# First block of a two-block model: another form of the block compression, another order of the attention scores, and earlier bias loads

## The chip, the cores and the metric

The kernel runs on one core of a Trainium2 chip. The metric is the time of one execution on the device, in microseconds (us). Lower is better. Engines are named as in the profile: PE is TensorE, DVE is VectorE, ACT is ScalarE, POOL is GpSimd, SP is SyncE, whose queue here only issues transfers.

## The reference

Two transformer blocks run one after the other over 256 tokens of width 1024, in float32. The first block has a modulation from a condition vector, an mLSTM with four heads, sparse attention with eight heads in two key groups, and a mixture of 32 experts of which each token uses four. The second block has 16 more tokens, differential attention, a recurrent branch and a dense feed-forward layer. The change touches the sparse attention of the first block and the biases of its experts:

```python
def compress(k, pos_emb, w):          # one key per 32 tokens, stride 16
    idx = jnp.arange(n_cmp)[:, None] * CMP_STRIDE + jnp.arange(CMP_BLOCK)[None, :]
    blocks = k[:, idx] + pos_emb[None, None, :, None, :]
    return jnp.einsum('bilgd,lde->bige', blocks, w)

# sparse attention: compressed keys, selected blocks and a window, each with a
# softmax over q.k * scale + position bias of the head; three gates add them up
lc = jnp.einsum('bqghd,bigd->bqghi', qq, kc) * scale + bias_c
lw = jnp.einsum('bqghd,bkgd->bqghk', qq, kwb) * scale + bias

# expert: up = x @ w_up + b_up, swiglu, down = act @ w_down + b_down
```

With 256 tokens every block is selected, so the selected and the window branch see all earlier tokens.

## The kernel before

The program is written once through a layer that gives each engine its own list of instructions. The order in a list is set by a scheduler from the order in the source, so that what stands next to what is read from the lists and not from the source. `mixer` computes the modulation (`modulate`), then runs the list `it` of `mixer_items` (attention, mLSTM, output projection), then `close_mixer` and `router`. `moe` follows with the experts, `block2` with the second block.

A projection is a product of float32 split into a high and a low part: ACT casts a weight piece to `wh`, DVE or POOL computes the rest `wl`, and TensorE does three passes per row tile (lines 339 to 341, or 365 to 367 where tokens stand still). `F(key, n, then)` is one such projection of 128 columns, 24 passes; pieces are split three ahead (`LEAD1`). Between the projections stand the small steps of the attention. All PSUM tiles come from one pool of eight banks.

- `cin(n)` lays the 16 token offsets of the keys (n = 0) or values (n = 1) into `kx`. `compress(n)` (line 599) takes 16 products with the 128x128 weight `wcmp` as stationary operand, and streams 32 columns of `kx`. The output columns stand twice in the weight. DVE copies the sum to `pcs` and adds the position term to get `kcT` (line 605). `values_c` (line 612) transposes the compressed value, `values_c2` (line 621) spreads it.
- `scores(h)` has two products for head h (lines 682 and 684), over 64 rows: heads 0 to 3 use the lower half of the rows, heads 4 to 7 the upper. DVE adds the position bias `bt` and takes the maximum (line 691, four pieces per head), ACT takes exponentials. `turn(h)` transposes them (lines 705 to 707), `outs(h)` multiplies with the values (lines 724, 726).
- `cmp_scores` (line 637) has the scores of the compressed keys, `cmp_turn` (line 662) their transpose.
- `flips` (line 489) turns the position bias into `bt`.
- `row1(n)` is a part of the modulation (`mod_part`, line 502): 8 products with 32 stationary columns, in four column groups.
- `bias_part(c)` (line 1109) loads a piece of the expert biases to `bx` with ACT's queue and splits it into three bfloat16 parts with four casts on ACT and two differences on DVE.

SP's queue issues all the large weights in order (line 225, `load_w`, five buffers of 2 MB; line 1092 for the experts). A load waits there until its buffer is free, and those behind it wait too.

Of the kernel before, what the change touches and what calls it, by code (L numbers as in the profile page):

```python
# [9 lines left out]
F32 = mybir.dt.float32  # L10
# [4 lines left out]
ALU = mybir.AluOpType  # L15
# [99 lines left out]
def host_layout(i):  # L115
# [47 lines left out]
    o["wcmp"] = np.concatenate([wc, wc], 4).reshape(P, 4096)  # L163
# [31 lines left out]
class Kernel:  # L195
# [215 lines left out]
    def modulate(self, pc):  # L411
# [3 lines left out]
        sel = self.selm = pa.tile([P, 12], F32, name="selm")  # L415
        nc.gpsimd.memset(sel, 0.0)
        for j in range(4):
            nc.gpsimd.affine_select(sel, sel, pattern=[[-1, 12]], compare_op=ALU.not_equal, fill=1.0, base=-32 * j,
                                    channel_multiplier=1)
# [90 lines left out]
    def mixer_items(self, sx):  # L510
# [64 lines left out]
        def keys(n):  # L575
            return lambda po: nc.scalar.copy(kk[:, n], po)
# [99 lines left out]
        def scores(h):  # L676
            g, j = h // 4, h % 4

            def f():
                s = slice(64 * g, 64 * g + 64)  # L680
                p1 = self.ps(f"ps_a{h}")
                nc.tensor.matmul(p1, qa[s, j, P:T1], kkf[s, :], start=True, stop=True)
                p0 = self.ps(f"ps_b{h}")
                nc.tensor.matmul(p0[:, :T1], qa[s, j, 0:P], kk[s, :, 0:P], start=True, stop=True)
                e = B["e", h] = tx(f"e{h}", [P, 768], "e", 2)
                mx = tx(f"mx{h}", [P, 2, 2], "mx", 2)
                sm = B["sm", h] = tx(f"sm{h}", [P, 2, 2], "sm", 4)
                pieces = [(p1, 256 * b, T1, 256 * b, 1, b, bt[:, h, :]) for b in range(2)]
                pieces += [(p0, 128 * b, P, 512 + 128 * b, 0, b, bt[:, h, P:T1]) for b in range(2)]
                for ps, po, w, o, tt, b, bias in pieces:  # L690
                    nc.vector.tensor_tensor_reduce(e[:, o : o + w], ps[:, po : po + w], bias, scale=1.0, scalar=NEG,
                                                   op0=ALU.add, op1=ALU.max, accum_out=mx[:, tt, b : b + 1])
                nc.vector.tensor_scalar(mx, mx, -1.0, None, op0=ALU.mult)
                for ps, po, w, o, tt, b, bias in pieces:
                    nc.scalar.activation(e[:, o : o + w], e[:, o : o + w], AF.Exp, bias=mx[:, tt, b : b + 1],
                                         accum_out=sm[:, tt, b : b + 1])
            return f
# [103 lines left out]

        def load_gains():
# [82 lines left out]
        def T(key, off, n, xs, then, order=tuple(range(KT))):  # L885
            return [p if i % 2 else p[:2] + (pool,) for i, p in enumerate(self.lin_t(key, off, n, xs, then, None, order))]
# [9 lines left out]
        it += T("wins", 0, 280, xs, values) + [self.flips] + F(W0, 0, keys(0)) + F(W0, 1, keys(1)) + [gates2, compress(1), values_c]  # L896
        it += F(W1, 0, queries(0)) + [compress(0), scores(0), values_c2] + F(W1, 1, queries(1)) + [scores(4), row1(4)]
        it += F(W1, 2, queries(2)) + [turn(0)] + F(W1, 3, queries(3)) + [cmp_scores, scores(1), turn(4)]
        it += F(W2, 0, qkin(0)) + [cmp_turn, scores(5)] + F(W3, 0, qkin(4)) + [cmp_out, turn(1), outs(0), outs(4), row1(5)]
        it += F(W2, 1, qkin(1)) + [scores(2), outs(1)] + F(W3, 1, qkin(5)) + [turn(5), scores(6), row1(6)]  # L900
        it += F(W2, 2, qkin(2)) + [outs(5), turn(2), scores(3)] + F(W3, 2, qkin(6)) + [outs(2), turn(6), scores(7)]
        it += F(W2, 3, qkin(3)) + [outs(6), turn(3)] + F(W3, 3, qkin(7)) + [decay(0), outs(3), row1(7)]
        it += so_[0:2] + [turn(7)] + so_[2:4] + [decay(1), outs(7)] + so_[4:8] + [row1(8)] + vm_[0:4] + [row1(9)]
        it += vm_[4:8] + [show, load_gains, mixed(0), decay(2), row1(10), mixed(1), decay(3), turn_cat(4), turn_cat(5)]
        it += [row1(11), mixed(2), turn_cat(6), turn_cat(7), rows, mixed(3), end_att, bias(0), rows2]
        it += [turn_cat(0), turn_cat(1), bias(1), turn_cat(2), turn_cat(3), row2(10), row2(11), load_x]
# [1109 lines left out]
```

## Time and profile before

| | |
|---|---|
| median of three runs | 1950.04 us (1944.28 to 1952.6) |
| profiled execution | 1948.96 us, span 1947.3 us |
| PE busy | 1746.0 us, 90% of the span |
| DVE, ACT, POOL busy | 811.6, 570.7, 264.4 us |
| DMA | 557.72 MB, mean 286 GB/s |
| granted TensorE clock, mean | 0.937 |

The first 260 us are the first block without its experts, up to about 1190 us the experts run, and then the second block. Busy shares over the whole span mix these three. A granted clock of 1.00 is 2.4 GHz, 0.50 is 1.2 GHz. Spans of matmuls are modelled and overlap, so the distance from one start to the next tells more than the length of one. The trace counts two passes for a float32 product, which the instruction lists count as one.

### The profile page before, as it was taken

Reading aid. Unit: us, or ns where it says so; the run is one execution under the profiler, and the core shown is the slowest. Engines: PE = TensorE matmul, PEld = TensorE weight load, DVE = VectorE, ACT = ScalarE, POOL = GpSimd, SP = SyncE. Lnnn points to the kernel's source line nnn. Section 1 sums busy time; section 2 is a strip of 40 time slices with the busy share of each in tenths; the row PEclk is TensorE's granted clock in tenths of the full one; section 3 lists DMA queues with packets and bytes.
Section 4 is the critical chain, followed back from the end, with each engine's and each line's share of the span. In section 5 each row is a group of like instructions: output and inputs, shape, how many; then the busy total and the mean of one; then the engine's idle time right before and its main releaser. Section 6 shows DMA issues by size and latency. Waiting matters only on the chain.

```text
span 1947.3 us, 34253 instructions
## 1 busy us (share of the span) xinstructions
PE 1746.0 (90%) x14547; PEld 1239.9 (64%) x14548; DVE 811.6 (42%) x1804; ACT 570.7 (29%) x1128; POOL 264.4 (14%) x259
## 2 busy tenths in 40 slices
PE   6999979965999997699999766979999999789998
PEld 3877743433543543354254434878999998789998
DVE  3364552211122222122121214577666557876653
ACT  3454521100111110011010102435444446354442
POOL 2213110000000000000000001051233102323320
PEclk7899989987999999899999977888999999799999
DMA  9447869999999999999999998210443452225441
GB/s 384 181 183 270 307 269 430 426 427 425 393 426 427 427 426 427 427 425 428 427 426 427 427 427 349 98 52 36 173 173 133 149 222 93 82 87 188 175 149 52
DMA packets 42697, 557.72 MB, mean 286 GB/s; under 512 B 4788, under 2 KB 5964, under 8 KB 8360
## 3 DMA queue, kind: packets, MB, share of 16 engines
q1 hardware_dynamic: 39920, 548.67, 68.7%
q0 software_dynamic: 1200, 4.29, 0.6%
q10 hardware_dynamic: 1416, 2.49, 0.4%
q8 instruction: 116, 1.90, 0.4%
q14 instruction: 45, 0.37, 0.1%
HBM read 554.37 MB, written 1.06 MB: 285 GB/s over the span
## 4 chain that ended last, share of the span: by engine, by line
PE 56%; DMA 12%; DVE 5%; ACT 1%; issue 1%; ACTq 0%; POOL 0%; DVEq 0%; POOLq 0%
DMA we<-wexp 12%; PE ps_lin L339 9%; PE ps_lin L340 9%; PE ps_lin L341 9%; PE ps_l L1293 6%; PE ps_u L1293 6%; PE ps_d L1293 6%; PE ps_g L1259 2%; PE ps_c L1356 2%; DVE qk L1765 1%; PE ps_at L1336 1%; PE nm0ss L1473 0%; PE ps_rqb L1784 0%; PE ps_ri L1659 0%; PE ps_pg L1321 0%
## 5 line engine op out<-in xcount | busy, mean ns | idle before, releaser
L339 PE MATMUL ps_lin<-xhi,wh 128*128 128x272 f32 (+1 forms) x1024 | 301.9, 295 | 0.5 <-ACT xhi L1403 0.5
L340 PE MATMUL ps_lin<-xlo,wh 128*128 128x272 f32 (+1 forms) x1024 | 298.0, 291 | 0.4 <-DVE xlo L1404 0.4
L341 PE MATMUL ps_lin<-xhi,wl 128*128 128x272 f32 (+1 forms) x1024 | 298.0, 291 | 0.0
L1293 PE MATMUL ps_d<-we,at 128*32 128x256 f32 (+1 forms) x2048 | 219.7, 475 | 47.6 <-DMA we<-wexp 38.1
L1293 PE MATMUL ps_l<-we,xg 128*32 128x256 f32 (+1 forms) x2048 | 214.0, 454 | 30.6 <-DMA we<-wexp 29.7
L1293 PE MATMUL ps_u<-we,xg 128*32 128x256 f32 (+1 forms) x2048 | 211.9, 452 | 29.1 <-DMA we<-wexp 29.1
L339 PEld LDWEIGHTS ps_lin<-xhi,wh 128*128 128x128 f32 x1024 | 198.0, 194 | 2.5 <-ACT xhi L1403 0.8
L340 PEld LDWEIGHTS ps_lin<-xlo,wh 128*128 128x128 f32 x1024 | 198.0, 193 | 0.9 <-DVE xlo L1404 0.6
L341 PEld LDWEIGHTS ps_lin<-xhi,wl 128*128 128x128 f32 x1024 | 198.1, 193 | 0.0
L1293 PEld LDWEIGHTS ps_d<-we,at 128*32 128x32 f32 (+1 forms) x2048 | 89.2, 126 | 163.8 <-issue 94.5
L1293 PEld LDWEIGHTS ps_l<-we,xg 128*32 128x32 f32 (+1 forms) x2048 | 87.4, 120 | 139.7 <-issue 92.4
L1293 PEld LDWEIGHTS ps_u<-we,xg 128*32 128x32 f32 (+1 forms) x2048 | 85.5, 120 | 132.7 <-issue 77.5
L1360 DVE TENSOR_TENSOR hT<-hT,ps_c 128x512 f32<-128x512 f32 x128 | 79.3, 682 | 131.7 <-PE ps_c L1356 131.7
L1379 POOL TENSOR_TENSOR hT<-hT,g 128x1024 f32<-128x1024 f32 x1 | 3.3, 3257 | 943.2 <-DVE ssm L1377 943.2
L1422 ACT CAST wh<-wgu 128x1024 fp32r<-128x1024 f32 x88 | 92.2, 1049 | 121.9 <-PE ps_lin L340 119.3
L1425 DVE TENSOR_TENSOR wl<-wgu,wh 128x1024 fp32r<-128x1024 f32 x88 | 108.2, 1231 | 41.9 <-ACT wh L1422 41.9
L1305 DVE TENSOR_SCALAR gl<-ps_u 128x512 f32<-128x512 f32 (+1 forms) x36 | 20.3, 572 | 222.1 <-PE ps_u L1297 222.1
L1337 ACT COPY at<-ps_at 128x512 f32<-128x512 f32 (+1 forms) x36 | 17.4, 493 | 305.7 <-PE ps_at L1336 304.9
L339 PE MATMUL ps_lin<-ahi,wh 128*128 128x272 f32 (+1 forms) x352 | 100.5, 286 | 0.0
L341 PE MATMUL ps_lin<-ahi,wl 128*128 128x272 f32 (+1 forms) x352 | 99.9, 284 | 0.0
L340 PE MATMUL ps_lin<-alo,wh 128*128 128x272 f32 (+1 forms) x352 | 99.8, 283 | 0.0
L1422 ACT CAST wh<-win 128x1024 fp32r<-128x1024 f32 (+1 forms) x72 | 60.9, 855 | 117.9 <-PE ps_lin L340 115.2
(675 smaller groups left out, 2931.5 us busy)
## 6 DMA issues: line engine op xcount, KB each, us to landing
we<-wexp SPq DMA_DIRECT2D x192, 2048.0 KB, 27.0
wgu<-wgu SPq DMA_DIRECT2D x22, 2048.0 KB, 7.8
win<-win SPq DMA_DIRECT2D x14, 2048.0 KB, 8.1
wada<-wada SPq DMA_DIRECT2D x12, 2048.0 KB, 8.3
wdn<-wdn SPq DMA_DIRECT2D x16, 1408.0 KB, 6.1
wout<-wout SPq DMA_DIRECT2D x6, 2048.0 KB, 7.7
wint<-wint SPq DMA_DIRECT2D x2, 2048.0 KB, 11.2
wcmpNone<-wcmp SPq DMA_DIRECT2D x1, 2048.0 KB, 22.7
```

Source lines behind the costliest of these rows:

```text
L339: nc.tensor.matmul(po[:m, :nn], hi[:, a], xh[k], start=(k == 0), stop=False)
L340: nc.tensor.matmul(po[:m, :nn], hi[:, a], xl[k], start=False, stop=False)
L341: nc.tensor.matmul(po[:m, :nn], lo[:, a], xh[k], start=False, stop=(k == nk - 1))
L1259: nc.tensor.matmul(p, self.x[:, tt, k * P : k * P + P], oh[:, tt], start=(tt == 0), stop=(tt == 1))
L1293: nc.tensor.matmul(dst[b][s], lhs(k, b), ws[k // 4][:, o : o + wd], start=(k == 0 and b % per == 0), stop=False)
L1305: nc.vector.tensor_scalar(gl[i], pu[i], 7.0, 0.5, op0=ALU.min, op1=ALU.mult)
L1336: nc.tensor.transpose(pt[:, c * P : c * P + P], li[i][:, c * P : c * P + P], self.ident)
L1356: nc.tensor.matmul(pc[s][:, (tt - t0) * wd : (tt - t0) * wd + wd], gt[b][rows[s], tt * P : tt * P + P], y[b // per][rows[s], (b % per) * w ...
L1360: nc.vector.tensor_tensor(a, a, pc[s].rearrange("p (a b) -> p a b", a=per), op=ALU.add)
L1422: nc.scalar.copy(hi, src)
L1425: nc.vector.tensor_tensor(lo, src, hi.bitcast(F32), op=ALU.subtract)
L1765: nc.vector.tensor_tensor(B["qk"][:, i], B["qk"][:, i], z, op=ALU.add)
```

## The change

- Compression: the weight `wcmp` no longer repeats its columns (1 MB and no longer 2). The 32 columns of `kx` are the stationary operand, the 64 output columns stream, and product l writes to the column group of 32 that l modulo 4 names. DVE copies the four partial sums, twice side by side, to `cp`. A new step `compress2` adds and transposes them with one product with the selection matrix `selm`, which is widened from 12 to 32 columns. From there on all is as before.
- Scores: `scores(j)` issues both products of head j and of head 4+j, first the two large ones, then the two small, and then their DVE and ACT steps. `e` has three buffers, not two.
- Biases: the six pieces are loaded by `load_bias(c)` into the memory of `bt` (four, by SP's queue) and further ones by ACT's queue, ahead of `bias_part`.
- The list `it` is ordered anew around these steps.

```diff
-    o["wcmp"] = np.concatenate([wc, wc], 4).reshape(P, 4096)
+    o["wcmp"] = wc.reshape(P, 2048)
...
         def compress(n):
...
                 for l in range(16):
-                    o = (n * 16 + l) * P
-                    nc.tensor.matmul(pc[:, 0:32], w[:, o : o + P], kx[:, n, l].rearrange("p g i -> p (g i)"),
-                                     start=(l == 0), stop=(l == 15))
+                    o = (n * 16 + l) * 64
+                    q = 32 * (l % 4)
+                    nc.tensor.matmul(pc[q : q + 32, 0:64], kx[:, n, l].rearrange("p g i -> p (g i)"), w[:, o : o + 64],
+                                     start=(l < 4), stop=(l >= 12))
+                cp = B["cp", n] = tx(f"cp{n}", [P, 2, 64])
+                nc.vector.tensor_copy(cp, pc[:, 0:64].unsqueeze(1).to_broadcast([P, 2, 64]))
+            return f
+
+        def compress2(n):
+            def f():
+                pc = self.ps(f"ps_cmt{n}")
+                nc.tensor.matmul(pc[:, 0:32], B["cp", n].rearrange("p a b -> p (a b)"), self.selm, start=True, stop=True)
...
+        def scores(j):
...
+                for g in range(2):
+                    s = slice(64 * g, 64 * g + 64)
+                    p1 = self.ps(f"ps_a{4 * g + j}")
+                    nc.tensor.matmul(p1, qa[s, j, P:T1], kkf[s, :], start=True, stop=True)
+                    pss.append([p1])
+                for g in range(2):
+                    s = slice(64 * g, 64 * g + 64)
+                    p0 = self.ps(f"ps_b{4 * g + j}")
+                    nc.tensor.matmul(p0[:, :T1], qa[s, j, 0:P], kk[s, :, 0:P], start=True, stop=True)
+                    pss[g].append(p0)
+                for g in range(2):
+                    h = 4 * g + j
...
+                    e = B["e", h] = tx(f"e{h}", [P, 768], "e", 3)
...
+        def load_bias(c):
+
+            def f():
+                self.bx[c] = b2[0:96, 512 * (c % 4) : 512 * (c % 4) + 512]
+                (nc.sync if c < 4 else nc.scalar).dma_start(self.bx[c], d["bexp"][:, c * 512 : c * 512 + 512])
+            return f
...
-        it += T("wins", 0, 280, xs, values) + [self.flips] + F(W0, 0, keys(0)) + F(W0, 1, keys(1)) + [gates2, compress(1), values_c]
-        it += F(W1, 0, queries(0)) + [compress(0), scores(0), values_c2] + F(W1, 1, queries(1)) + [scores(4), row1(4)]
+        it += T("wins", 0, 280, xs, values) + [self.flips] + F(W0, 0, keys(0)) + [compress(1)] + F(W0, 1, keys(1))
+        it += [gates2, compress2(1), compress(0), values_c]
+        it += F(W1, 0, queries(0)) + [compress2(0), scores(0), values_c2] + F(W1, 1, queries(1)) + [row1(4)]
...
     def bias_part(self, c):
...
-            b = self.pr.tile([96, 512], F32, name=f"bx{c}", tag="bx", bufs=2)
+            b = self.bx[c]
...
-            nc.scalar.dma_start(b, self.d["bexp"][:, c * 512 : c * 512 + 512])
```

On PE, between the key projections and the first query projection, before the change (`ps_ac` is the gates' transpose, `ps_cmp` the compression, `ps_vc` the compressed value's transpose, `ps_lin` the projection):

```order
L565 MATMUL ps_ac<-ident,mr 128x4
L599 MATMUL ps_cmp_671<-cat,wcmpNone 128x32 x16
L612 MATMUL ps_vc<-ident,kcT 16x128
L339 MATMUL ps_lin_702<-hhi,wh_614 128x256
L340 MATMUL ps_lin_702<-hlo,wh_614 128x256
```

and with the change (`ps_cmt` is the selection product of `compress2`):

```order
L565 MATMUL ps_ac<-ident,mr 128x4
L610 MATMUL ps_cmt_690<-selm,cp_648 128x32
L601 MATMUL ps_cmp_696<-wcmpNone,cat 32x64 x16
L622 MATMUL ps_vc<-ident,kcT 16x128
L339 MATMUL ps_lin_725<-hhi,wh_614 128x256
L340 MATMUL ps_lin_725<-hlo,wh_614 128x256
```

The values' compression moved forward, to the second key projection (one of its 16 products among that projection's first passes, 15 before the next projection), and the keys' compression took its place.

On PE, between the first and the second query projection, before the change (`ps_a` and `ps_b` are a head's scores, `ps_rv` is `values_c2`):

```order
L599 MATMUL ps_cmp_732<-cat,wcmpNone 128x32 x16
L682 MATMUL ps_a_753<-kk,qa 128x512
L684 MATMUL ps_b_755<-kk,qa 128x256
L621 MATMUL ps_rv<-vc,rep 128x128
L339 MATMUL ps_lin_778<-hhi,wh_648 128x256
```

and with the change:

```order
L610 MATMUL ps_cmt_755<-selm,cp_713 128x32
L693 MATMUL ps_a_761<-kk,qa 128x512
L693 MATMUL ps_a_763<-kk,qa 128x512
L698 MATMUL ps_b_765<-kk,qa 128x256
L698 MATMUL ps_b_767<-kk,qa 128x256
L631 MATMUL ps_rv<-vc,rep 128x128
L339 MATMUL ps_lin_802<-hhi,wh_667 128x256
```

Head 4 moved to head 0. Pairs (2, 6) and (3, 7) stand in the same way; in pair (1, 5) four products of `cmp_scores` stand after the first `ps_a` and five of `mod_part` before the second `ps_b`.

In SP's queue, from the mLSTM's weights (`wint`) on, with the change (`wada` is the modulation, `wout` the output projection; before the change the rows are the same without line 824):

```order
L225 DMA wint1_120<-wint 128x4096
L824 DMA bt_140<-bexp 96x512 x2
L225 DMA wint0_124<-wint 128x4096
L225 DMA wada8_126<-wada 128x4096
L225 DMA wada7_122<-wada 128x4096
L824 DMA bt_140<-bexp 96x512 x2
L225 DMA wada9_128<-wada 128x4096
L225 DMA wada11_132<-wada 128x4096
L225 DMA wada10_130<-wada 128x4096
L225 DMA wout0_134<-wout 128x4096
```

Four bias loads moved into this queue from ACT's.

## Rows read from the trace of the kernel before

**Rows 1.** Busy time by stage; columns: stretch, length, each engine, granted clock, DMA.

```profile
94.30:160.00 65.70, 64.88 (x477) 51.58 (x477) 43.60 (x157) 36.06 (x107) 14.05 (x11) 1.00 0.51 197
160.00:250.00 90.00, 89.03 (x505) 66.46 (x503) 46.03 (x113) 47.26 (x91) 21.66 (x19) 0.96 0.73 275
250.00:260.00 10.00, 1.49 (x6) 1.35 (x6) 9.04 (x74) 1.30 (x4) 6.83 (x36) 0.50 0.14 42
260.00:1190.00 930.00, 810.31 (x7692) 387.31 (x7696) 196.49 (x431) 108.30 (x269) 0.00 (x0) 0.94 1.00 423
1190.00:1947.30 757.30, 705.40 (x5430) 678.73 (x5427) 482.62 (x941) 341.03 (x578) 196.62 (x144) 0.95 0.35 130
```

**Rows 2.** Waits, PE 72 to 260 us and SP's queue: total us, times, longest.

```profile
PE ps_rank L996 <- DVE sel L989: 7.7, 1, 7.7
PE ps_pc L662 <- DVE lc L657: 0.8, 1, 0.8
...
SPq L1092 <- DVE gate L1002: 20.4, 1, 20.4
```

**Rows 3.** Busy time of projections before and after the first compression, columns as above.

```profile
66.00:72.00 6.00, 6.00 (x50) 5.74 (x48) 1.37 (x2) 2.92 (x6) 1.91 (x3) 1.00 0.99 403
77.45:82.60 5.15, 5.15 (x25) 5.15 (x26) 0.97 (x2) 0.62 (x1) 0.00 (x0) 0.50 0.00 0
...
89.90:94.30 4.40, 4.40 (x26) 4.17 (x25) 1.81 (x6) 2.49 (x9) 1.33 (x2) 0.67 0.71 302
```

**Rows 4.** PE's timeline around the compressions: start, length, line, product, shapes, passes, wait.

```profile
72.45 4.09 PE L599 MATMUL ps_cmp<-cat,wcmpNone 128*128 128x32 f32 x32
77.42 0.37 PE L612 MATMUL ps_vc<-ident,kcT 128*16 128x128 f32 x1 [0.89 <-DVE kcT L605]
...
82.65 3.85 PE L599 MATMUL ps_cmp<-cat,wcmpNone 128*128 128x32 f32 x32
86.43 2.07 PE L682 MATMUL ps_a<-kk,qa 64*128 64x512 f32 x2
...
89.28 0.79 PE L621 MATMUL ps_rv<-vc,rep 16*128 16x128 f32 x2
```

**Rows 5.** PE's timeline, scores of head 2 and what follows.

```profile
127.73 1.12 PE L682 MATMUL ps_a<-kk,qa 64*128 64x512 f32 x2
...
129.22 0.88 PE L724 MATMUL ps_y<-vs,pr 128*128 128x64 f32 x6
```

**Rows 6.** PE's timeline of other forms, and loads of L502 (ns min/median/max).

```profile
62.84 3.60 PE L489 MATMUL ps_fl<-hank,flip 128*128 128x512 f32 x8
...
104.23 0.96 PE L637 MATMUL ps_cx<-kcT,qa 64*128 64x16 f32 x14
...
120.98 0.78 PE L724 MATMUL ps_y<-vs,pr 128*128 128x64 f32 x6
...
177.19 0.39 PE L366 MATMUL ps_lin<-wl,hhi 128*128 128x512 f32 x1
177.41 0.39 PE L367 MATMUL ps_lin<-wh,hlo 128*128 128x512 f32 x1
177.73 1.92 PE L502 MATMUL ps_modr<-wada,sc 128*32 128x512 f32 x16
...
L502 PEld LDWEIGHTS ps_modr<-wada,sc x128: 106/110/110, 95.8 to 201.1; 128*32 128x32 f32 x128
```

**Rows 7.** Waits of PE from 0 to 72 us, and PE's timeline at 193 us.

```profile
PE ps_mod L502 <- DMA wada<-wada: 2.7, 3, 1.5
PE ps_lin L366 <- DVE wl L1427: 1.5, 2, 1.0
...
192.85 3.63 PE L502 MATMUL ps_modr<-wada,sc 128*32 128x512 f32 x30
```

**Rows 8.** DVE's instructions of L691 (ns min/median/max, first and last start, form).

```profile
L691 DVE CUSTOM_DVE_ANT_0 e<-ps_a,bt x16: 408/420/425, 88.5 to 151.5; 128x256 f32<-128x256 f32 x16
L691 DVE CUSTOM_DVE_ANT_0 e<-ps_b,bt x16: 276/286/292, 89.4 to 152.4; 128x128 f32<-128x128 f32 x16
```

More of the change, by code (lines that the diff above doesn't have):

```diff
@@ L674, in mixer_items @@
         kkf = kk.rearrange("p b t -> p (b t)")
-        def scores(h):
-            g, j = h // 4, h % 4
+        def scores(j):
             def f():
[L680 to L696, printed above, removed]
@@ new lines, in f @@
+                pss = []
+                for g in range(2):
[8 more added lines that the diff above has]
+                    pss[g].append(p0)
@@ new lines, in f @@
+                for g in range(2):
+                    h = 4 * g + j
+                    p1, p0 = pss[g]
+                    e = B["e", h] = tx(f"e{h}", [P, 768], "e", 3)
+                    mx = tx(f"mx{h}", [P, 2, 2], "mx", 2)
+                    sm = B["sm", h] = tx(f"sm{h}", [P, 2, 2], "sm", 4)
+                    pieces = [(p1, 256 * b, T1, 256 * b, 1, b, bt[:, h, :]) for b in range(2)]
+                    pieces += [(p0, 128 * b, P, 512 + 128 * b, 0, b, bt[:, h, P:T1]) for b in range(2)]
+                    for ps, po, w, o, tt, b, bias in pieces:
+                        nc.vector.tensor_tensor_reduce(e[:, o : o + w], ps[:, po : po + w], bias, scale=1.0, scalar=NEG,
+                                                       op0=ALU.add, op1=ALU.max, accum_out=mx[:, tt, b : b + 1])
+                    nc.vector.tensor_scalar(mx, mx, -1.0, None, op0=ALU.mult)
+                    for ps, po, w, o, tt, b, bias in pieces:
+                        nc.scalar.activation(e[:, o : o + w], e[:, o : o + w], AF.Exp, bias=mx[:, tt, b : b + 1],
+                                             accum_out=sm[:, tt, b : b + 1])
@@ L800, in mixer_items @@
         grow = {4: kk.rearrange("p a b -> p (a b)"), 5: vs.rearrange("p a b -> p (a b)")}
+        def load_bias(c):
[3 more added lines that the diff above has]
+            return f
+        self.bx = {}
         def load_gains():
@@ L900, in mixer_items @@
[L900 to L903, printed above, removed]
+        it += T("wins", 0, 280, xs, values) + [self.flips] + F(W0, 0, keys(0)) + [compress(1)] + F(W0, 1, keys(1))
@@ new lines, in mixer_items @@
+        it += [gates2, compress2(1), compress(0), values_c]
+        it += F(W1, 0, queries(0)) + [compress2(0), scores(0), values_c2] + F(W1, 1, queries(1)) + [row1(4)]
+        it += F(W1, 2, queries(2)) + [turn(0)] + F(W1, 3, queries(3)) + [cmp_scores, turn(4), scores(1)]
+        it += F(W2, 0, qkin(0)) + [cmp_turn, turn(1)] + F(W3, 0, qkin(4)) + [cmp_out, outs(0), outs(4), row1(5)]
+        it += F(W2, 1, qkin(1)) + [scores(2), turn(5), outs(1)] + F(W3, 1, qkin(5)) + [row1(6), turn(2)]
+        it += F(W2, 2, qkin(2)) + [outs(5), turn(6), scores(3)] + F(W3, 2, qkin(6)) + [outs(2), outs(6)]
@@ L904, in mixer_items @@
+        it += F(W2, 3, qkin(3)) + [turn(3)] + F(W3, 3, qkin(7)) + [decay(0), outs(3), row1(7)]
+        it += so_[0:2] + [turn(7)] + so_[2:4] + [decay(1), outs(7)] + [load_bias(c) for c in range(4)] + so_[4:8] + [row1(8)] + vm_[0:4] + [row1(9)]
         it += vm_[4:8] + [show, load_gains, mixed(0), decay(2), row1(10), mixed(1), decay(3), turn_cat(4), turn_cat(5)]
         it += [row1(11), mixed(2), turn_cat(6), turn_cat(7), rows, mixed(3), end_att, bias(0), rows2]
-        it += [turn_cat(0), turn_cat(1), bias(1), turn_cat(2), turn_cat(3), row2(10), row2(11), load_x]
+        it += [turn_cat(0), turn_cat(1), load_bias(4), bias(1), turn_cat(2), turn_cat(3), load_bias(5), row2(10), row2(11), load_x]
```

6 lines of the change are left out of this document (2 added, 4 removed).

## The prediction, made before the changed kernel ran

> **What bounds the kernel now.** I read the program by stages first. From 260 to 1190 us the DMA share is 1.00 at 423 GB/s: the experts' weights set the pace there, and TensorE waits for them. From 1190 us on TensorE is busy 705 of 757 us. Neither stage is touched by the change beyond a few neighbours trading places, so I count both as fixed lengths that begin when the stage before them lets them [rows 1]. What lets them begin is the router: the queue that issues the expert weights stood 20.4 us waiting for the gates, and the DMA share is 0.14 just before they come [rows 1, 2]. The first block is therefore in series with all the rest: a microsecond taken off it is a microsecond off the end.
>
> Inside the first block TensorE is the limit. From 94.3 to 250 us it is busy 154 of 156 us [rows 1], and the waits say the same: 0.8 us for the compressed scores, then 7.7 us for the router's choice, which is the end of the block [rows 2]. So each step of the change is priced by the TensorE time it takes away or adds before 250 us.
>
> The clock comes with it. The projection products run at one pass per 0.120 us (50 in 6.00) at a granted clock of 1.00, which is 2.4 GHz. Right after the first compression the granted clock is 0.50, 1.2 GHz, and a pass takes 0.206 us (25 in 5.15) [rows 3]. What TensorE did before each fall was a compression: 32 passes, each with a load of 128 columns for a stream of only 32.
>
> **The change part by part.** *Compression.* Before, the first compression with the wait behind it lasts from 72.45 to 77.42, 4.97 us, 0.89 of it the wait for the key that VectorE finishes. The second lasts from 82.65 to 86.43, 3.78 us [rows 4]. That is 8.75 us. Now the 16 products of each have the 32 tokens as stationary operand, stream 64 columns, and stand in four column groups. The trace counts two passes per float32 product, so there are 8 rounds of four. A round costs at least its stream: 512 columns take 3.60/8 = 0.45 us, so 64 take 0.056 and a compression 0.45 us. If the groups did not overlap, 32 loads of 0.110 us would give 3.5 us. The nearest row is the modulation, also 32 stationary columns in four groups: 16 passes of 512 columns in 1.92 us, where 0.45 each would be 7.2, so the groups do overlap [rows 6]. A load (0.110) outlasts the 0.056 stream, so I take 0.11 per round, 0.9 us per compression. Each then needs one product with the selection matrix, two passes with 128-column loads at 4.09/32 = 0.13 us [rows 4], 0.26 us. Going into the column groups costs 0.32 - 0.23 = 0.09 us (177.41 to 177.73, against 0.23 between the passes before; [rows 6]). The new order has six such borders, 0.5 us, because one product of the first compression stands alone among the key products. New total: 1.8 + 0.5 + 0.5 = 2.8 us, a gain of 5.9. Ends: 6.8 if only the stream counts, 0.8 if nothing overlaps. The wait of 0.89 us I count as gone: the second compression (0.9 us) now stands between the selection product and the transpose that needs its key. Without that cover it is back.
>
> The Trainium skill, "TensorEngine Tiling (Array Packing)", Key Properties, says that a change of tiling mode drains the engine, which speaks against splitting a compression. The 0.09 us of the trace is what that drain costs here, and the sum has it. "TensorE: Matmul & The Clock Gate", LDWEIGHTS, gives a load as its columns over 1.2 GHz, which would be 27 ns for 32 columns. The trace has 106 to 110 ns for float32 [rows 6]. By the page the gain would be near the upper end, 6.8.
>
> *The clock.* If it stays at 1.00, the query products behind the first compression gain 25 x (0.206 - 0.120) = 2.15 us and the 26 passes from 89.9 to 94.3 gain 4.40 - 3.12 = 1.28 [rows 3]. The first head's score products take 89.28 - 86.43 = 2.85 us there, and 129.22 - 127.73 = 1.49 at full clock [rows 4, 5], another 1.36. Sum 4.8. I expect it to stay. The products with 64-column streams on the whole array (6 in 0.78 us, [rows 6]) sit in a stage whose granted clock is 1.00 throughout [rows 1], and the new compression streams 64 columns for 0.9 us at a time. Ends: 0 if it falls as now, and -2 if the early first compression makes it fall among the key products, which have the full clock today.
>
> *Scores in pairs.* A head's two products take 1.49 us on half of the rows [rows 5]. Heads j and 4+j lie on different halves. Products that alternate between the halves go 14 passes in 0.96 us, 0.069 each, against 0.13 for passes with the same load on all rows [rows 6], so they do run side by side. In the new order three of the four pairs stand next to each other, and each saves 1.49 us: 4.5. The pair (1, 5) has compressed scores and modulation products in between, and I give it nothing. Ends: 0 and 6.
>
> *Bias loads.* Two of six stood first in ScalarE's queue and ran among the first block's weights. 0.39 MB at 0.423 MB/us [rows 1] is 0.9 us of DMA time, and TensorE waits 2.7 us for those weights [rows 7], so I take 0.9 (0 to 0.9). Four now stand in SP's queue and wait until VectorE has read the position bias. Behind the last two stand three modulation weights, both output weights and the experts'. VectorE's last such read starts at 152.4 [rows 8], and the modulation that is first among those held is needed at 192.85 [rows 7], so nothing is late. The 24 bias casts on ScalarE are the same ones, 16 of them now before the output weights' casts. ScalarE is busy 47 of 90 us there [rows 1]: nothing, or up to 2 us if the output product has to wait for a cast.
>
> *Flips.* Two of the four bias flips now stand among the value products, where TensorE waits 1.5 us for VectorE's splits [rows 7]. I take 0.5 (0 to 1.5).
>
> *New waits.* A pair gives VectorE 4 x 0.42 + 4 x 0.29 = 2.8 us in one piece, where it had 1.4 [rows 8]. Behind it are the splits that the next projection needs, and behind the exponentials the transposes, which for heads 1 and 2 now come one projection (3 us) after their scores. VectorE is busy 43.6 of 65.7 us in that stage [rows 1], and the stage gets shorter. Ends: 0, and 1.4 us at each of four pairs, 5.6. I take 1.5, nearer to none, since splits are made three parts ahead.
>
> Sum: 5.9 + 4.8 + 4.5 + 0.9 + 0.5 - 1.5 = 15.1 us. The profiled execution took 1948.96 us, 1.08 below the median of 1950.04. That gives 1933.9 in its terms and 1934.9 in the median's: **1935 us**.
>
> **Rivals.** *The clock falls all the same.* For it: products over only 64 rows and short streams remain near the compression. Against it: the stage of the other short streams keeps 1.00. Then 4.8 are missing: 1940.
>
> *VectorE takes over.* Both ends of the new waits' term: 4 us more, 1939. For it: the long pieces. Against: it has a third of the stage free.
>
> *The groups don't do what they say.* If passes in different column groups run one after the other, a compression stays at 3.5 us, 5.1 of the 5.9 go, and the clock goes with them, since its cause is back: 15.1 - 5.1 - 4.8 = 5.2, 1945. Against it stands the modulation's row.
>
> *Slower than before: starved pairs.* If TensorE waits at the pairs and the clock falls after each, a fall costs about 2.2 us (its price after the first compression) and a wait about 1.4. Four pairs and two compressions make 6 x 3.6 = 21.6 us, against a gain of 15.1 - 4.8 + 1.5 = 11.8 without the clock and without the waits: 1960. It decides from the fourth such place on (14.4). Against it: the clock holds 1.00 from 94.3 to 160 today with a wait of 0.8 us inside.
>
> **How the numbers follow.** About 0.5% is what a measurement of this kernel can tell from no change: 9.7 us, so a time below 1940.3 counts as faster. My forecast (1928 to 1939) has 0.60. The clock's fall has 0.16, half of it on either side of the bound. VectorE has 0.09, two thirds on the faster side. Groups that don't overlap have 0.10, all within 0.5%. Starved pairs have 0.05. Faster: 0.60 + 0.08 + 0.06 = 0.74, less 0.02 for a forecast that ends just short: 0.72. Same 0.23, slower 0.05. The range is 1926 to 1944: its low end has pair (1, 5), the flips and the loads at their best ends, and its high end takes in the clock, VectorE and most of the way to the groups.
>
> **What would show it.** In the profile after, the two compressions together below 2.5 us, and the granted clock at 1.00 between about 72 and 95 us, show the first two steps right. The score products of a pair starting within 0.1 us of each other, and four of them ending in about 1.6 us, show the third. The router's wait should come about 15 us earlier with the expert stage and the second block as long as before. If TensorE waits more than 5 us for VectorE or ScalarE between 90 and 150 us, the new-waits term was too small. If the first block is shorter by 15 us and the end is not, the premise that the rest only shifts was wrong.

## The result, and the profile after

The changed kernel takes 1936.13 us against 1950.93 for the kernel before, a ratio of 0.9925 (95% interval 0.991 to 0.9941), 14.8 us less. A second series (label after_again, below) gave 0.9911 (0.9888 to 0.9934). The prediction was 1935 with a range from 1926 to 1944, so time, range and sign were right. Several steps behind them were not. Times and ratios leave out one execution of the version with whole runs (2196.9 us, at a granted clock of 0.734 instead of 0.94).

The stages of the profiled execution, in the columns of [rows 1]:

```profile
core 0 of [0], span 1936.1 us
72.00:95.00 23.00, 21.11 (x205) 17.40 (x204) 12.06 (x39) 11.22 (x32) 8.23 (x7) 1.00 0.72 280
85.00:145.00 60.00, 60.00 (x462) 48.73 (x458) 39.75 (x148) 35.45 (x107) 14.05 (x11) 1.00 0.58 217
145.00:236.60 91.60, 90.53 (x503) 68.06 (x502) 45.11 (x113) 46.54 (x91) 21.83 (x19) 0.94 0.73 273
236.60:246.60 10.00, 1.49 (x6) 1.35 (x6) 9.01 (x75) 1.34 (x4) 6.80 (x36) 0.50 0.14 42
246.60:1180.00 933.40, 817.16 (x7704) 391.26 (x7707) 196.63 (x431) 108.34 (x269) 0.00 (x0) 0.93 1.00 422
```

From 72 to 95 us the granted clock is now 1.00, where [rows 3] had 0.50 and 0.67. The router's stretch of 10 us with the clock at 0.50 and 1.49 us of TensorE comes 13.4 us earlier than in the third row of [rows 1]. The experts' stage behind it has the same DMA rate (422 GB/s, 423 before).

TensorE's timeline around the compressions, which answers [rows 4] and [rows 5] (start, length, line, product, shapes, passes, wait):

```profile
65.55 0.30 PE L601 MATMUL ps_cmp<-wcmpNone,cat 128*32 128x64 f32 x2
...
68.49 0.65 PE L601 MATMUL ps_cmp<-wcmpNone,cat 128*32 128x64 f32 x30
...
72.43 0.41 PE L610 MATMUL ps_cmt<-selm,cp 128*128 128x32 f32 x2
72.77 0.65 PE L601 MATMUL ps_cmp<-wcmpNone,cat 128*32 128x64 f32 x32
...
74.52 0.27 PE L622 MATMUL ps_vc<-ident,kcT 128*16 128x128 f32 x1 [1.10 <-DVE kcT L615]
...
77.37 0.30 PE L610 MATMUL ps_cmt<-selm,cp 128*128 128x32 f32 x2
...
78.46 1.13 PE L693 MATMUL ps_a<-kk,qa 64*128 64x512 f32 x4 [0.79 <-ACT qa L579]
79.43 0.60 PE L698 MATMUL ps_b<-kk,qa 64*128 64x256 f32 x4
79.96 0.37 PE L631 MATMUL ps_rv<-vc,rep 16*128 16x128 f32 x1
```

A compression of 32 passes lasts 0.65 us. The two heads of the first pair take 1.50 us (78.46 to 79.96), as long as one head took in [rows 5]. Two waits stand in brackets, 1.10 us at the transpose of the compressed values and 0.79 us at the first pair. They are the only ones of the attention, as the waits of TensorE from 66 to 250 us show (total, times, longest, as [rows 2]; the first row is the router's choice, the second lies in the experts' stage):

```profile
PE ps_rank L1024 <- DVE sel L1017: 7.7, 1, 7.7
PE ps_g L1286 <- issue: 1.8, 1, 1.8
PE ps_vc L622 <- DVE kcT L615: 1.1, 1, 1.1
PE ps_a L693 <- ACT qa L579: 0.8, 1, 0.8
```

Stage lengths follow from the starts of TensorE's first products: of a projection, of the mLSTM's output (`ps_n`, line 779 of the kernel before; the output projection begins some 20 us later), of the router's ranking, of the residual. The last stage ends with the start of TensorE's last product, 5 to 6 us before the span's end. In us, two profiled executions of each kernel:

| stage | before | changed |
|---|---|---|
| start, to the first projection | 42.6, 44.1 | 43.1, 41.1 |
| first block, to the mLSTM's first output product | 153.9, 155.1 | 138.3, 138.4 |
| output stage: mLSTM's output and output projection, up to the ranking | 60.4, 61.9 | 62.1, 62.1 |
| experts, up to the residual | 936.3, 936.3 | 939.1, 935.9 |
| second block | 748.7, 748.7 | 747.7, 747.7 |

The first block lost 16 us. In the two first profiles the execution is only 11.1 us shorter (1948.96 to 1937.82), because the experts and the output stage are longer there. By the means the other four stages together lose nothing, and the start and the experts differ as much between two executions of one program as between the kernels.

### The profile page after: what moved, and what is told of

It reads as the page before. It is cut to its first block, busy times and chain, and to the rows that moved or that the text cites. A ratio compares the mean times of both kernels' runs of the same rounds, so it can differ in the third digit from the quotient of the medians.

```text
span 1936.1 us, 34266 instructions
## 1 busy us (share of the span) xinstructions
PE 1739.4 (90%) x14551; PEld 1231.3 (64%) x14552; DVE 810.0 (42%) x1806; ACT 568.3 (29%) x1127; POOL 264.4 (14%) x259
## 4 chain that ended last, share of the span: by engine, by line
PE 56%; DMA 12%; DVE 5%; ACT 1%; issue 0%; ACTq 0%; POOL 0%; DVEq 0%; POOLq 0%
DMA we<-wexp 12%; PE ps_lin L339 9%; PE ps_lin L340 9%; PE ps_lin L341 9%; PE ps_l L1320 7%; PE ps_u L1320 6%; PE ps_d L1320 6%; PE ps_g L1286 2%; PE ps_c L1383 2%; DVE qk L1792 1%; PE ps_at L1363 1%; PE ps_rqb L1811 0%; PE ps_ri L1686 0%; PE ps_pg L1348 0%; PE nm0ss L1500 0%
## 5 line engine op out<-in xcount | busy, mean ns | idle before, releaser
L1288 ACT ACTIVATE xg<-ps_g,modc,a2c 128x128 f32<-128x128 f32 (+1 forms) x120 | 43.8, 452 | 171.0 <-PE ps_g L1286 171.0
```

The source lines that it names most:

```text
L1288: nc.scalar.activation(xg[:, k], pg[:, (k - k0) * n : (k - k0) * n + n], AF.Identity, scale=self.a2c[:, k : k + 1], bias=self.modc2[:, k : ...
```

## The experiments

For each, the time in the first block is split by product, each product counted from its start to the next one's, so that a wait belongs to the product ahead of it. "Half clock" is how much of the block had the granted clock at 0.50. Of it, 4.6 to 6.5 us lie at the block's start in every kernel. The last row is the second block, measured as above.

| us in the first block | before | loads alone | compression undone | pairs undone | changed | one group | whole runs, again |
|---|---|---|---|---|---|---|---|
| label | | c_bias | u_compress | u_pairs | | a1_one_group | v_whole_again |
| projections | 88.9 | 87.0 | 86.2 | 84.7 | 84.2 | 85.0 | 84.4 |
| compression, selection, transpose | 8.8 | 8.3 | 8.6 | 4.0 | 4.0 | 5.3 | 2.3 |
| scores of heads | 12.9 | 11.6 | 7.8 | 11.6 | 6.5 | 6.5 | 6.0 |
| modulation | 16.6 | 16.5 | 15.7 | 14.6 | 17.6 | 15.7 | 14.7 |
| whole block | 153.9 | 150.0 | 145.1 | 140.9 | 138.3 | 138.1 | 132.8 |
| half clock | 19.5 | 12.6 | 15.4 | 8.7 | 5.4 | 6.5 | 4.7 |
| second block | 748.7 | 744.5 | 745.1 | 748.8 | 747.7 | 740.9 | 745.6 |

No edit names the second block, yet its length moves by up to 8 us from one version to another, as much as the steps under test. It goes with the order that the scheduler made there: with the pairs undone TensorE's order in it is that of the kernel before, and so is its length (748.8 and 748.7). Two executions of one program agree within 0.1 us, but for the whole runs (747.8 and 745.6). So the times and ratios below hold the effect of that order too, and what an edit did in the first block is read from the table.

**Compression undone.** The old `compress` (128 columns loaded, 32 streamed) in the old places, with the old weight of 2 MB and the old selection matrix, all else as changed.

```diff
-                    nc.tensor.matmul(pc[q : q + 32, 0:64], kx[:, n, l]..., w[:, o : o + 64], start=(l < 4), stop=(l >= 12))
+                    nc.tensor.matmul(pc[:, 0:32], w[:, o : o + P], kx[:, n, l]..., start=(l == 0), stop=(l == 15))
```

> The changed kernel with the compression alone undone (128 columns loaded for each 32-column stream, at the old places; pairs and bias loads as changed). Theory: the parts add up, and the pairs with the flips are worth about 5 us of the 14.8: ratio to the kernel before 0.997 (1945), a compression of some 3.8 us again, and the granted clock at 0.50 behind each. Rival 1: the pairs only pay when the first block is short, so alone they give nothing: 1.000 (1951). Rival 2: the pairs carry most of the gain: 0.994 or lower.

Measured: 1939.98 us, ratio 0.9946 (0.9929 to 0.9963). A compression lasts 3.76 and 3.97 us again, and the clock is at 0.50 behind each (stages, columns of [rows 1]):

```profile
68.00:73.00 5.00, 5.00 (x45) 4.78 (x43) 0.87 (x2) 1.01 (x3) 1.38 (x2) 1.00 0.60 256
73.80:79.00 5.20, 5.07 (x24) 5.10 (x25) 0.97 (x2) 0.62 (x1) 0.00 (x0) 0.50 0.00 0
...
83.80:86.00 2.20, 2.20 (x9) 0.83 (x5) 1.03 (x6) 0.00 (x0) 0.00 (x0) 0.50 0.86 216
```

So the old form of the compression brings the falls back. But the rest kept 10.7 us, not 5: close to rival 2's number, though not for its reason. The first block gives 8.8 us of it, 5.1 in the scores, and the second block, in another order, 3.6. The loads alone, below, are 10 us faster too.

**Pairs undone.** One head at a time in the old order, two buffers for `e`, the rest as changed.

```diff
-        def scores(j):
+        def scores(h):
...
-    [..., scores(0), values_c2] + F(W1, 1, queries(1)) + [row1(4)]
+    [..., scores(0), values_c2] + F(W1, 1, queries(1)) + [scores(4), row1(4)]
```

> The changed kernel with the pairs alone undone (one head's scores at a time in the old order, with two buffers for the exponentials; compression and bias loads as changed). Theory: compression and clock together are worth about 10 us: ratio 0.995 (1941), granted clock 1.00 from 72 to 95 us, compressions of 0.65 us. Rival: the score products of a single head, on half of the rows, make the clock fall once the compression no longer does: 4 us less gain, 0.997 (1945).

Measured: 1935.51 us, 0.9934 (0.9911 to 0.9957). The scores cost 11.6 instead of 6.5 us, so the pairs do save 5.1 there. The two times can't be told apart (0.9925 for the changed kernel). The block is only 2.6 us longer than the changed kernel's, since the modulation is 3.0 us cheaper. TensorE's timeline says why. The changed kernel's modulation of the attention stage, with its neighbours:

```profile
95.87 0.59 PE L693 MATMUL ps_a<-kk,qa 64*128 64x512 f32 x1
96.39 1.90 PE L502 MATMUL ps_modr<-wada,sc 128*32 128x512 f32 x10
98.23 0.70 PE L698 MATMUL ps_b<-kk,qa 64*128 64x256 f32 x2
...
105.50 1.05 PE L502 MATMUL ps_modr<-wada,sc 128*32 128x512 f32 x2
106.48 0.70 PE L679 MATMUL ps_oc<-vblk,pct 128*128 128x512 f32 x1
...
111.02 1.05 PE L502 MATMUL ps_modr<-wada,sc 128*32 128x512 f32 x4
112.00 0.39 PE L339 MATMUL ps_lin<-hhi,wh 128*128 128x256 f32 x1
...
117.23 1.92 PE L502 MATMUL ps_modr<-wada,sc 128*32 128x512 f32 x14
...
123.44 1.05 PE L502 MATMUL ps_modr<-wada,sc 128*32 128x512 f32 x2
```

and the same 32 passes with the pairs undone:

```profile
97.51 3.64 PE L502 MATMUL ps_modr<-wada,sc 128*32 128x512 f32 x32
```

The passes run four at a time in column groups. A run of 2 or 4 passes still occupies 0.98 us up to the next product (105.50 to 106.48, 111.02 to 112.00), one of 10 or 14 occupies 1.84 or 1.85 (96.39 to 98.23, 117.23 to 119.08). In all traces, at full clock and where no wait follows, runs of 2 to 8 passes take 0.98 to 1.00 us and runs of 10 to 16 take 1.83 to 1.85. So a cut costs when it makes more sets of up to eight passes (four products), and costs nothing between two full sets: two runs of 16 take 3.7 us, one of 32 takes 3.6. Cut in five runs, two parts cost 6.6 us instead of 3.6.

The theory's granted clock of 1.00 up to 95 us didn't hold: it fell for 3.4 us at 92.3 us, among the products of the compressed scores. Such a fall comes back below in one execution of a version with all pairs whole, so this run doesn't show that single heads cause it, as the rival has it.

**One column group.** All 16 products of a compression in the first group.

```diff
-                    q = 32 * (l % 4)
+                    q = 0
...
-                                     start=(l < 4), stop=(l >= 12))
+                                     start=(l == 0), stop=(l == 15))
...
```

> The changed kernel with the 16 products of a compression in one column group in place of four (same stationary tokens, same 64-column streams, same output). Theory: the four groups overlap and this is where the 0.65 us come from; in one group each of 32 passes costs its load of 0.11 us, 3.5 us a compression, 5.7 us more in all, and the long stretch of small passes makes the clock fall again, 4.8 us more: 1946.5, ratio 0.9975. Rival 1: loads hide behind the streams of 0.056 us, a compression takes 1.8 us, the clock stays: 1938.5, ratio 0.994. Rival 2: 3.5 us a compression and the clock stays at 1.00, since it was the 128-column loads that made it fall: 1942, ratio 0.9953.

Measured: 1932.38 us, 0.9906 (0.9887 to 0.9926), and no fall of the clock between the compressions and the last turns.

```profile
75.67 0.38 PE L610 MATMUL ps_cmt<-selm,cp 32*128 32x32 f32 x2
75.98 1.97 PE L601 MATMUL ps_cmp<-wcmpNone,cat 128*32 128x64 f32 x32
77.88 0.28 PE L622 MATMUL ps_vc<-ident,kcT 128*16 128x128 f32 x1
```

32 passes in 1.97 us, a new one every 0.056 us, and the clock stays: rival 1. Its time was 6 us too high (1938.5). The second block, in another order, is 6.8 us shorter here than in the changed kernel. The load of 32 columns lasts 0.11 us in its record, but another starts before it ends, so it doesn't pace the passes. In four groups the same passes take 0.65 us (a round of four starts every 0.056 us), so the groups do overlap, and are worth 1.3 us a compression. Of the 2.6 us for two, the block shows 1.3 (5.3 against 4.0), because the longer second compression covers the wait at the transpose (no bracket in the last row). The modulation stands in 8 runs here instead of 10, and so the two blocks are equally long. The exchange of the operands, not the groups, is what took away most of the compression's time (8.8 to 5.3 us) and the falls. The old form differs from this one both in its load and stream and in its length (4.09 against 1.97 us); which of them makes the clock fall stays open.

**The addition that reads PSUM.**

```diff
-                    nc.vector.tensor_scalar(kcT[s, n], pcs[s, 16 * g : 16 * g + 16], ...
+                    nc.vector.tensor_scalar(kcT[s, n], pc[s, 16 * g : 16 * g + 16], ...
```

> The changed kernel with one operand changed: the addition that finishes the compressed key reads its input from PSUM instead of the copy in SBUF. Theory: the 1.1 us wait at the transpose of the compressed values is GpSimd's: the addition, 0.23 us otherwise, lasts 1.03 us and ends with the 1.27 us split that GpSimd runs at that moment. With PSUM as the source it lasts 0.23 us beside the same split, and the wait is 0.3 us. Rival: the wait is the chain of VectorE steps between the selection product and the transpose, whatever they read, and stays above 0.9 us.

Measured, in one profiled execution of 1938.67 us. First the changed kernel, then this one (timeline of VectorE, GpSimd, TensorE):

```profile
72.83 1.27 POOL L1454 TENSOR_TENSOR wl<-win,wh 128x512 fp32r<-128x512 f32 x1 [2.30 <-PE ps_cmt L610]
73.10 1.27 DVE L615 TENSOR_SCALAR kcT<-pcs 64x16 f32<-64x16 f32 x2
```

```profile
73.55 1.27 POOL L1454 TENSOR_TENSOR wl<-win,wh 128x512 fp32r<-128x512 f32 x1 [2.30 <-PE ps_cmt L610]
73.81 0.48 DVE L615 TENSOR_SCALAR kcT<-ps_cmt,pcs 64x16 f32<-64x16 f32 x2
...
74.44 0.27 PE L622 MATMUL ps_vc<-ident,kcT 128*16 128x128 f32 x1 [0.31 <-DVE kcT L615]
```

The two additions take 0.48 us beside the same GpSimd split, and the wait falls from 1.10 to 0.31 us. So 0.8 us of the wait was GpSimd's hold on VectorE, as the theory said. The Trainium skill, "SBUF — State Buffer", section "SBUF: two separate sides", has this rule: VectorE and GpSimd share a pair of ports; of a GpSimd instruction and a VectorE instruction of a kind that needs the pair, the one that starts first holds it for its whole length, and the other stands still. The trace agrees: the first of the two additions that read SBUF ends at 74.13 us, the split, which began first, at 74.10. But one addition of the second compression also ended with its split (79.50 and 79.47 us), though by the records it began 0.03 us before it, which the rule doesn't give.

**The loads alone, twice.** The kernel before with `load_bias` alone.

```diff
-            nc.scalar.dma_start(b, self.d["bexp"][:, c * 512 : c * 512 + 512])
...
-    ... [decay(1), outs(7)] + so_[4:8] ...
+    ... [decay(1), outs(7)] + [load_bias(c) for c in range(4)] + so_[4:8] ...
-    ... [turn_cat(0), turn_cat(1), bias(1), turn_cat(2), turn_cat(3), row2(10), ...
+    ... [turn_cat(0), turn_cat(1), load_bias(4), bias(1), turn_cat(2), turn_cat(3), load_bias(5), row2(10), ...
```

> The kernel before with the bias loads alone changed (four on SP's queue behind the last outputs of the heads, two on ScalarE's later, into tiles that exist already). Theory: 0 to 0.9 us at the start, and the first block, from its first projection product to its first output product, as long as before, 153.9 us; the expert stage, from the router's ranking to the residual products, 2 to 3 us longer than before (939 instead of 936), because the four loads now run in the queue that issues the expert weights, which all three kernels with the change of the bias loads show. Ratio 1.000 to 1.001. Rival: the longer expert stage is chance or belongs to the earlier router, so that it is 936 here, and the ratio is 0.9995.

> The kernel before with the bias loads alone changed, once more for its stages. Its first timing was 10 us below the kernel before, of which its profile has 4 us in the first block, all while the granted clock is at 0.50, and 4 us in the second block, 2 of them a wait of 1.7 us for ScalarE at the squared norms that the new order there doesn't have. Theory: the 2 us of the second block are the order's and come again; the shorter falls behind the compressions are chance, and here they last 13 us or more in all as in the kernel before: first block 153 us. Rival: the falls are short again (7 us, first block 150 us), so they go with the loads.

Measured: 1943.49 us, 0.9952 (0.9936 to 0.9968), some 10 us less where a ratio of 1.000 to 1.001 was expected. The profiled repeat took 1943.53 us. One part is sound. The waits at the modulation weights and at the splits are shorter in both executions (TensorE up to 100 us, against [rows 7]; 1.8 and 1.4 us in the second execution of the kernel before):

```profile
PE ps_mod L502 <- DMA wada<-wada: 1.2, 1, 1.2
...
PE ps_lin L366 <- DVE wl L1435: 0.5, 1, 0.5
```

The flips moved too (the first from 62.8 to 56.9 us). The second block is 744.5 and 744.4 us where the kernel before has 748.7. Its longest waits, before and here, show some 1.5 us of that: a wait of 1.7 us for ScalarE that the order there no longer has, and small differences in two others.

```profile
PE ps_rot L1763 <- ACT z L1748: 5.7, 2, 4.1
PE ps_rqb L1784 <- DVE rq_y L1777: 5.4, 1, 5.4
PE ro03r L1449 <- DVE ro_y L213: 2.0, 1, 2.0
PE ps_qs L1760 <- ACT qsq L1750: 1.7, 1, 1.7
```

```profile
PE ps_rqb L1792 <- DVE rq_y L1785: 5.9, 1, 5.9
PE ps_rot L1771 <- ACT z L1756: 5.4, 3, 4.1
PE ro03r L1457 <- DVE ro_y L213: 2.0, 1, 2.0
```

The scheduler rebuilt the second block's order although the change doesn't name it. The first block was 150.0 us in one execution and 152.5 in the other, with falls of 3.4 and 6.8 us behind each compression (6.8 and 6.8, 6.8 and 10.2 in the two executions of the kernel before). So the same program has falls of either length, as the second expectation's theory has it. By the means of two executions each, the start gives 1.1 us, the first block 3.3 (1.0 of it the splits' waits), the output stage 1.0 and the second block 4.3, and the experts take 1.0 back: 8.7 of the 10. From the first block on and without the experts, 11.0 us less pass at half clock, so by an estimate some 5.5 of the 8.7 are falls of the clock, 2.7 of them in the first block. Whether the loads have a part in the shorter falls, or these executions were lucky, stays open.

**The experts' stage.** It was 2 to 3 us longer in the first profiles with the change.

```diff
-                (nc.sync if c < 4 else nc.scalar).dma_start(self.bx[c], ...
+                nc.scalar.dma_start(self.bx[c], ...
```

> The changed kernel with all six bias loads on ScalarE's queue, none on SP's. Theory: the expert stage is back at 936 us, 2.7 us less: 1933.4, ratio 0.991, as long as the loads' wait for VectorE's reads doesn't hold up ScalarE in the first block (then up to 2 us are lost again). Rival: the expert stage stays at 939 us and the ratio at 0.9925.

> The kernel before once more, for its stages: how far the start, the first block, the expert stage and the second block differ between two executions of the same program. Theory: first block within 1 us of 153.9 us, expert stage 936 us as in the first profile. Rival: the expert stage lasts 939 us here too, so its 2.7 us are no part of the change.

> The changed kernel once more, beside the version with whole modulation runs on the same chip. Theory: the first block, from the first projection product to the first output product, within 1.5 us of 138.3 us, with no fall of the granted clock between the compressions and the last turns, and a ratio of 0.9925 to the kernel before. Rival: the first timing was on the slow side, since versions with the same first block came out at 0.988 to 0.991: then 0.990.

The stage is 938.6 us without any load on SP's queue, 937.3 twice with the loads alone, 936.3 again in the kernel before, and 939.1 and 935.9 in the two executions of the changed kernel (942.0 in the version whose addition reads PSUM, which has the same loads). The same program differs by 3.2 us here, so no run shows that the queue makes the stage longer, and the first expectation fell. The 1929.43 us of the kernel without loads on SP's queue, ratio 0.9882 (0.9864 to 0.9901), have other sources in its trace: its first block is 135.7 us, with the modulation in 8 runs (15.7 us) instead of 10, its output stage 60.4 us and its second block, in another order, 745.9. The kernel before, once more, has a first block of 155.1 us, 0.2 us outside the 1 us that was expected. The changed kernel, once more, has 138.4 us without a fall there, as expected; its ratio of 0.9911 lies between the theory's 0.9925 and the rival's 0.990, and the interval holds both.

**The two waits covered, then whole runs.**

```diff
-        it += [gates2, compress2(1), compress(0), values_c]
-        it += F(W1, 0, queries(0)) + [compress2(0), scores(0), values_c2] + F(W1, 1, queries(1)) + [row1(4)]
+        it += [gates2, compress2(1)]
+        it += F(W1, 0, queries(0)) + [compress(0), values_c, scores(0)] + F(W1, 1, queries(1)) + [compress2(0), values_c2, row1(4)]
```

and, in the second of them, `[cmp_scores, turn(4), row1(5), scores(1)]`, with `row1(5)` gone from behind `outs(4)`; both read the key's addition from PSUM.

> A further version of the changed kernel: the second compression, the transpose of the compressed values and the first pair stand behind both query projections' first part, the key's last addition reads PSUM instead of SBUF. Theory: the two waits that the trace of the changed kernel shows in the first block, 1.1 us at the transpose and 0.8 us at the first pair, go, and nothing is late in their place: 1.9 us less, ratio 0.9915 (1934.2). Rival: the first pair's long piece of VectorE work now delays the splits of the next projection, and the time stays at 0.9925.

> The version without the two waits (label v_both), with the second modulation part moved ahead of the second pair. In that version's trace the modulation passes of the first block stand in 10 runs and last 17.1 us, where the kernel with undone pairs has 6 runs and 14.6 us: a run of 2 passes lasts 0.98 us, one of 16 lasts 1.85. Here they stand in 7 runs, and all four pairs are whole. Theory: a split costs the rounds that its passes no longer share, so three runs fewer give 2.5 us, and the second pair, whole, gives 1.4 us: first block 134.1 instead of 138.0 us, ratio 0.9866. Rival: the modulation weights arrive too late for the earlier place, TensorE waits for the DMA there, and nothing is gained: 0.9886.

> The version with whole modulation runs and whole pairs once more. Its profile has a first block of 134.8 us, 3.4 less than the changed kernel. Theory: it is faster than the changed kernel on the same chip by 3 to 5 us, ratio to the kernel before 0.988. Rival: what it wins in the first block is lost to falls of the clock behind it, and the two have the same time.

Covered waits: 1929.1 us, 0.9886 (0.9866 to 0.9906), 5 us below the expected 1934.2. Neither wait is left, and compression, selection and transpose cost 2.3 us. But the profiled first block was only 0.3 us shorter (138.0), because the clock fell at the second pair, and its second block, in another order, was 3.2 us shorter (744.5). So the time doesn't show what covering the waits is worth; the table's row for the compression does.

```profile
90.76 1.51 PE L647 MATMUL ps_cx<-kcT,qa 64*128 64x16 f32 x24
...
92.79 0.62 PE L647 MATMUL ps_cx<-kcT,qa 64*128 64x16 f32 x8
93.71 1.99 PE L693 MATMUL ps_a<-kk,qa 64*128 64x512 f32 x4
```

The four passes of the second pair's longer products took 1.99 us; at full clock the changed kernel's first pair's four take 1.13 and one head's two 1.12 [rows 5].

Whole runs: 0.9883 (0.9864 to 0.9902), then 0.9887 (0.986 to 0.9913), with first blocks of 134.8 and 132.8 us and the modulation at 16.4 and 14.7 us. The first of the two had a fall at the modulation ahead of the second pair. The second had a new wait of 0.6 us, at a turn for ScalarE's exponentials. The theory's 134.1 us for the block lies between the two; its 0.9866 is below both ratios, though inside both intervals. Beside the changed kernel on the same chip it was 1928.92 against 1933.12 us, 4.2 us less, as expected. The intervals of the two ratios overlap, so in time it is not shown to beat the changed kernel, though it does beat the kernel before.

## Why the prediction was right, step by step

The first block carried the prediction, and it gave 15.6 us in the two first profiles, where the steps that lie in it gave 14.2. The main mechanisms came out, but that the sum is so close is in part luck: misses of 0.4 to 1.5 us in its terms cancelled.

- **Compression: 5.9 predicted, 4.8 measured** (8.8 to 4.0, the 0.79 us of the next point included). Two errors against each other. A round was taken at 0.11 us, the length of a load; a round starts every 0.056 us, so a compression costs 0.65 us instead of 0.9, and the two with the selections cost 2.1 us of their own instead of 2.8. But the wait that was counted as gone is still there: 1.10 us instead of 0.89. The named cover did stand between product and transpose. What failed is the premise that VectorE finishes the key in the time it took in [rows 4]'s wait; beside a GpSimd split one addition takes 1.03 us.
- **New waits: 1.5 predicted, none where expected.** The splits and the turns behind the pairs wait for nothing. The 0.79 us stand at the first pair instead, for the query cast that the old compression used to cover. The prediction moved that compression and didn't ask what else it had hidden.
- **Clock: 4.8 predicted, about 5.7 measured.** Projections and flips went from 92.0 to 86.4 us, of which the splits' waits give 1.2 (1.8 to 0.6 us) and the clock 4.4. The eight heads cost 12.9 us against 8 x 1.49 = 11.9 at full clock, another 1.0, and the small products behind them 0.3. From 72 us to the last turn the granted clock stayed at 1.00, as "I expect it to stay" had it, and the undone compression brought the falls back.
- **Pairs: 4.5 predicted, 5.4 measured in the scores** (11.9 to 6.5): three pairs at 1.5 us and 1.0 from the split pair (1, 5), which was given nothing. What the step lacked is the price of what splits it. The changed order cuts the modulation in 10 runs instead of 8. That is 1.0 us more than before, where 0.8 us of the modulation's time was the wait for the compressed scores [rows 2], 1.9 more than in other versions with 8 runs (15.7), and 3.0 more than with the pairs undone (6 runs). The products of the compressed scores, cut up by the same pair, cost another 0.4 us (2.0 to 2.4). The order that the prediction had listed puts modulation products inside the pair; it read there only what that meant for the pair.
- **Loads and flips: 1.4 predicted.** The flips' 0.5 were 1.2 (the loads alone give 1.0 of it; the flips moved in that version too). The start's 0.9 can't be told from its spread (42.6 and 44.1 before, 43.1 and 41.1 after). That the loads alone give 10 us in the timings is the largest miss. That it didn't harm the sum is luck. Some 2.7 us of it are falls in the first block, which the changed kernel's other steps remove anyway. The shorter output stage and second block aren't there in the changed kernel, whose order is another (62.1 us, not 60.2, and 747.7, not 744.5).
- **"The rest only shifts" held to about 1 us a stage by the means.** The output stage has a longer fall of the clock (10.2 us in both executions; 6.8 and 10.2 before), the experts differ by 3.2 us between two executions of it, and the second block's order changed. In the experiments the second block's length moved by up to 8 us with its order. That it is 747.7 us here, near the 748.7 of before, is luck: the prediction counted on a few neighbours trading places.

Of the rivals, the falling clock, VectorE taking over and the starved pairs didn't come. "The groups don't do what they say" was priced wrongly: one group costs 1.97 us a compression, not 3.5, and doesn't bring the clock's fall back, so that rival's 1945 could not have come about.

## What to carry over

When a step is moved or shortened, list every wait that it used to cover, not only the one the change names: here the query cast was hidden by the old compression. Products that share rounds in column groups should be cut only behind a full set, one product in each of the four groups; each further set cost 0.9 us, more than the broken pair (1, 5), which cost 0.5 (scores of 6.5 against 6.0 us with all pairs whole). An experiment that undoes one part should be read by stage and by product, since the scheduler reorders stages that the edit doesn't touch: here the second block alone moved by up to 8 us.

## What the runs showed of the hardware

- A float32 load of 32 columns is recorded with 0.11 us, but passes with such loads start every 0.056 us in one column group, and rounds of four passes start every 0.056 us in four. The record's length is not its price. The Trainium skill, "TensorE: Matmul & The Clock Gate", LDWEIGHTS, would make it 27 ns, an estimate from its rule of columns over 1.2 GHz; no row here shows that figure, and the 64-column stream alone accounts for the 0.056 us.
- A VectorE addition of 64x16 elements that reads SBUF lasted 1.03 to 1.32 us beside a GpSimd split and 0.23 to 0.24 beside the same split when it read PSUM. One that reads SBUF and began 0.08 us before its split lasted 0.23 us (one column group, 81.49 us).
- The granted clock fell to 0.50 after 32 passes that each load 128 columns for a 32-column stream, in every profile with the old compression, and in three profiles at or just after the 32 passes of 16 columns of the compressed scores (pairs undone, covered waits, whole runs), but not in the second execution of the whole runs. After 32 passes of 64 columns in 0.65 or 1.97 us it never fell. How long a fall lasted differed between executions of one program by up to 3.4 us.
